# A hybrid decoder layer on one core: seven products for every pair of the MLP's second product, 13 pairs' weight sums made earlier, source order from the 19th early product

## The chip, the core and the metric

The kernel runs on one NeuronCore of a Trainium2 chip. The metric is device microseconds of one execution. TensorE (PE) does the matrix products, VectorE (DVE), ScalarE (ACT) and GpSimd (POOL) the elementwise work, and SyncE (SP) issues all DMAs of this kernel in one queue. PEld is the loading of TensorE's stationary operand.

## What is computed

One decoder layer on x (1024 tokens x 1024 features, float32): an input projection, a dilated attention in three head groups beside an RWKV-7 time mixing, a gated merge of the two with an output projection, and then, where the change mostly lies, a squared-ReLU MLP, with RMSNorm before and after each part:

```python
f = rmsnorm(h, ffn_pre_norm[i])
f = jnp.square(jax.nn.relu(f @ w_ff_in[i])) @ w_ff_out[i]      # 1024x1024 @ 1024x4096, then @ 4096x1024
h = h + rmsnorm(f, ffn_post_norm[i])
e = (p[i] @ w_ple[i]) * jax.nn.sigmoid(h @ w_ple_gate[i])
h = h + rmsnorm(e, ple_post_norm[i])
```

## The kernel before, in words

**Products in three passes.** A float32 operand x is split into a rounded high part and the rest: ACT copies x into a reduced-precision tile (the "high"), and DVE or POOL subtracts it from x (the "low"). A product is then high x high + high x low + low x high, three matmuls (`mm3`, lines 310, 312 and 314). So each operand costs one ACT copy and one subtraction beside PE's work, and a "low" is a subtraction of 128x512 elements with both inputs in SBUF.

**Stages, in order of time.** (1) the input projection and the RWKV recurrence; (2) the attention, whose chain of scores (`sc`), row maxima and exponentials (DVE writes `SB` and `ast`, ACT does the exp), transposes (`pt`), copies (`PB`) and values (`po`) runs through 24 rounds, while PE fills the time between with the input projection's remaining products (`z<-uh,wh`); (3) `combine` of the three groups and the `merge` of eight column blocks; (4) the output projection (`out_0`, `out_1`); (5) 32 "early" products of the MLP's first product (`early`), with preparation beside them (`beside`); (6) the pairs; (7) the tail: the last part of the second product, the embedding gate, the output.

**The pairs.** The MLP's inner width of 4096 is cut into NP = 16 pairs of 128 features (256 rows of w_ff_out each). In stage 6, loop index p runs from 1 to 15. In each step PE does the first product of pair p (five products of 12 matmuls, in 20 chunks of three, function `first`; tiles `z`), and between these chunks the second product of pair e = p-1. Its 2x2 blocks are multiplied in one of two ways. For even e, `seven`: seven products of block sums in place of eight (84 matmuls), accumulated in PSUM banks (`chain`), each of whose four banks DVE adds into the totals `tot` after each product: 28 evictions. For odd e, `plain`: all eight block products (96 matmuls), summed two by two in PSUM: 16 evictions. `seven` needs sums of blocks of its activations (`operand`, four DVE subtractions or additions of tile `hr` into tile `sum`), and sums of blocks of its weights. The weight sums of a pair are four DVE operations, then split (four ACT copies, four DVE lows) and stored in DRAM scratch (`bs`, 512 KB each, 4 for each pair); `fetch` loads them into `duo` when they are due. The pairs in `AHEAD = (4, 2, 0)` have them made beside the early products (`ahead_`), the other even ones beside the plain pair in front of them (`w2_sums` in the loop). In a plain pair DVE also makes four lows of the activations (`duo<-hr`), and ACT and POOL split the whole weights (`ws`).

Each step of the loop also loads one pair's w_ff_out rows (`load_w2`), the four blocks of the next w_ff_in pair (`w1_raw`), and the early products from scratch (`take`, tile `hr`), and POOL makes four sums of blocks of w_ff_in (`w1_sum`; tiles `wr`, `wl`) and five lows (`w1_split`). In plain pairs it also converts weights for the tail (`part`: tile `gp`, one DVE low and two stores for each of 28 halves).

**What sets the order.** PE's instructions are in source order throughout; a planner (`Order`) that runs while the program is written chooses when each generator of work goes on. It has a clock of its own, and spawned generators come in when it has passed the time that they yielded. For the other engines, `tc.manual_schedule(engines=...)` keeps source order while it is entered; outside it, the framework's scheduler orders their instructions. Before the change, all from the attention to the end of stage 5 is outside it (SP alone is in source order in stage 5), and all engines are in source order from the start of stage 6. `pend` and `flush` hold small jobs, lows above all, back to the next chunk.

**Buffers.** A tile is allocated by tag, and a new tile of the same tag waits until the old one is no longer read. The tag MP holds one 512 KB tile, BK2 a 1 MB one. PSUM has eight banks: s0, z0, z1 for `z`, and s1, s2, s3, m0, m1 for the rest; `bank(tags)` takes them in turn.

## Time and profile before

| | us |
|---|---|
| median of 3 runs (lowest to highest) | 1753.67 (1752.29 to 1756.36) |
| the profiled execution itself | 1755.44 |
| its span in the trace | 1753.7 |
| PE busy, DVE busy, ACT busy, POOL busy | 1727.1, 1108.6, 736.9, 606.0 |

The stages by the trace: the first attention transposes stand at 530.2, the merge's first product with the attention's result at 821.6, the output projection starts at 883.8, the early products at 974.4, the pairs at 1098.1, and the tail at 1608.4. A row of a group tells the line (118 is the helper that records every elementwise operation, so tiles tell more than lines), the engine, the operation, output tiles <- input tiles, the shape and the count, then busy time and the mean of one in ns, then the engine's idle time before them and who ended it. A row of the timeline tells the start and the duration in us, then the same, and in brackets the idle time before it. A row of the windows tells each engine's busy time in a stretch, the granted clock of TensorE as a share, the DMA engines' busy share and GB/s.

### The profile page before, as it was taken

The numbers are of one execution on the slowest core, as the hardware profiler recorded it, in microseconds if no ns is written. First come the engines' busy times: TensorE is split into PE (matmuls) and PEld (weight loads), VectorE is DVE, ScalarE is ACT, GpSimd is POOL, SyncE is SP. The second block draws the span as 40 slices with busy tenths as digits, with TensorE's granted clock in tenths as the row PEclk, the third lists the DMA queues.
The fourth block names the chain that finished last, engine by engine and source line by source line (L and its number), as shares of the span: only waits on it lengthen the run. The fifth ranks groups of instructions, "written<-read, shape, count | busy, mean of one in ns | idle before, by whom it ended". The sixth has DMA issues, their size and how long they took to land.

```text
span 1753.7 us, 26435 instructions
## 1 busy us (share of the span) xinstructions
PE 1727.1 (98%) x10132; PEld 1409.0 (80%) x10132; DVE 1108.6 (63%) x1926; ACT 736.9 (42%) x1353; POOL 606.0 (35%) x393
## 2 busy tenths in 40 slices
PE   9999999999999999999999998999999999999998
PEld 8777888887887777777788876888888888888887
DVE  6377778677654333445746752766788788787643
ACT  5823333241424443453444555333433443443354
POOL 1121110121122322323230346656656756752311
PEclk9999999999999999999999999999999999999999
DMA  4521121221333222234533386364464665567611
GB/s 164 214 84 37 67 79 62 84 73 63 107 115 107 85 61 61 73 117 147 192 100 120 120 334 237 129 219 157 145 245 175 203 223 174 194 225 273 221 49 49
DMA packets 99968, 244.77 MB, mean 140 GB/s; under 512 B 11393, under 2 KB 11777, under 8 KB 99330
## 3 DMA queue, kind: packets, MB, share of 16 engines
q1 hardware_dynamic: 99842, 243.08, 40.3%
q8 instruction: 80, 1.31, 0.3%
q14 instruction: 46, 0.38, 0.1%
HBM read 169.24 MB, written 67.11 MB: 135 GB/s over the span
## 4 chain that ended last, share of the span: by engine, by line
PE 80%; DVE 7%; ACT 4%; DMA 4%; issue 2%; POOL 2%; SPq 1%; DVEq 0%; ACTq 0%; POOLq 0%
PE z L310 15%; PE z L314 15%; PE z L312 15%; PE bk L310 8%; PE bk L314 8%; PE bk L312 8%; PE tp L301 1%; PE sc L293 1%; PE A L293 1%; PE po L293 1%; PE pt L301 1%; PE wr L293 1%; PE fq L293 1%; DVE duo L118 1%; POOL wl L118 1%
## 5 line engine op out<-in xcount | busy, mean ns | idle before, releaser
L118 POOL TENSOR_TENSOR wl<-wr,wh 128x1024 fp32r<-128x1024 f32 (+1 forms) x56 | 133.3, 2382 | 589.8 <-ACT wh L118 584.4
L310 PE MATMUL z<-uh,wh 128*128 128x512 f32 (+1 forms) x800 | 313.4, 392 | 4.0 <-DVE v L118 3.2
L312 PE MATMUL z<-ul,wh 128*128 128x512 f32 (+1 forms) x800 | 312.6, 391 | 1.3 <-DVE ul L118 1.3
L314 PE MATMUL z<-uh,wl 128*128 128x512 f32 (+1 forms) x800 | 312.9, 391 | 0.7 <-POOL wl L118 0.7
L118 DVE TENSOR_TENSOR tot<-tot,bk 128x512 f32<-128x512 f32 x333 | 219.6, 681 | 82.3 <-PE bk L314 82.1
L310 PEld LDWEIGHTS z<-uh,wh 128*128 128x128 f32 x800 | 151.0, 189 | 36.0 <-issue 4.9
L314 PEld LDWEIGHTS z<-uh,wl 128*128 128x128 f32 x800 | 151.1, 189 | 31.8 <-issue 3.7
L312 PEld LDWEIGHTS z<-ul,wh 128*128 128x128 f32 x800 | 151.1, 189 | 31.7 <-issue 3.3
L118 ACT ACTIVATE wh<-wr 128x1024 fp32r<-128x1024 f32 (+2 forms) x94 | 81.0, 862 | 119.5 <-PE z L312 65.9
L118 ACT ACTIVATE hr<-hr 128x512 f32<-128x512 f32 x96 | 60.7, 632 | 134.8 <-DVE hr L118 133.3
L310 PE MATMUL bk<-duo 128*128 128x512 f32 x224 | 88.4, 395 | 0.3
L312 PE MATMUL bk<-duo 128*128 128x512 f32 x224 | 87.7, 392 | 0.0
L314 PE MATMUL bk<-duo 128*128 128x512 f32 x224 | 87.5, 391 | 0.0
L314 PE MATMUL bk<-ws,duo 128*128 128x512 f32 x224 | 87.1, 389 | 0.0
L310 PE MATMUL bk<-ws,duo 128*128 128x512 f32 x224 | 87.1, 389 | 0.0
L312 PE MATMUL bk<-ws,duo 128*128 128x512 f32 x224 | 87.1, 389 | 0.0
L118 ACT ACTIVATE duo<-sum 128x512 fp32r<-128x512 f32 x64 | 39.7, 628 | 112.4 <-DVE sum L118 100.5
L310 PE MATMUL z<-f,wh 128*128 128x512 f32 x212 | 83.1, 392 | 3.5 <-ACT pa L118 3.5
L314 PE MATMUL z<-f,wh 128*128 128x512 f32 x212 | 83.4, 393 | 1.3 <-POOL wh L118 1.3
L312 PE MATMUL z<-f,wh 128*128 128x512 f32 x212 | 83.0, 391 | 0.0
L118 POOL TENSOR_TENSOR wh<-wr,wh 128x512 fp32r<-128x512 f32 x38 | 54.5, 1437 | 81.2 <-ACT wh L118 81.2
L118 DVE TENSOR_TENSOR hr<-hr,z 128x512 f32<-128x512 f32 x80 | 54.5, 681 | 23.4 <-PE z L314 23.3
(371 smaller groups left out, 4009.2 us busy)
## 6 DMA issues: line engine op xcount, KB each, us to landing
wr<-in_wz_dram SPq DMA_DIRECT2D x48, 512.0 KB, 4.0
w2r<-in_w_ff_dram SPq DMA_DIRECT2D x34, 512.0 KB, 4.5
bs<-duo SPq DMA_DIRECT2D x32, 512.0 KB, 4.8
duo<-bs SPq DMA_DIRECT2D x32, 512.0 KB, 4.3
wr<-in_wff_dram SPq DMA_DIRECT2D x56, 256.0 KB, 3.6
hr<-p1scr SPq DMA_DIRECT2D x48, 256.0 KB, 4.1
xt<-in_x_dram SPq DMA_DIRECT2D x16, 512.0 KB, 3.9
gscr<-gst SPq DMA_DIRECT2D x32, 256.0 KB, 2.2
```

Source lines behind the costliest of these rows:

```text
L118: return f(*a, **kw)
L293: PE.matmul(out_, a, b, start=start, stop=stop)
L301: PE.transpose(out_, a, ident if idn is None else idn)
L310: PE.matmul(ps, ah, bh, start=start and i == 0, stop=False, skip_group_check=not start)
L312: PE.matmul(ps, ah, bl, start=False, stop=False, skip_group_check=not start)
L314: PE.matmul(ps, al, bh, start=False, stop=i == n - 1, skip_group_check=not start)
```

## The change

All pairs 0 to 14 of the second product are done by `seven`; `plain`, its weights' split and its branch of the loop are gone. So weight sums are needed for 15 pairs, not 8. `AHEAD` is now (1, 0): these two are made beside the early products. The other 13 (`SOONER`, pairs 2 to 14) are made by a new generator, `sooner`, which runs beside the attention. It loads each pair's two rows blocks again into one BK2 tile, and has 52 steps, for which it asks the planner for 5.0 us each (`PACE`): one or two DVE sums, one ACT copy into a tile of tag MP, one DVE low and one store of 512 KB. It writes to the engines directly, so that the planner's account of DVE's and ACT's time does not hold these operations. The tiles `rooms` for operands go round three pairs of buffers without a break. `part` comes twice in each step. Source order for DVE, ACT, POOL and SP begins at the 19th early product (j = 18), not at the first pair. In the early products' preparation, lows are made at once or at the end of the step. In `merge`, the blocks from j = 2 on take turns in four PSUM banks in place of two.

```diff
-LEAD, SPARE, LAG, HELD = 0.4, 0.5, 0.4, 2.5
+LEAD, SPARE, LAG, HELD, PACE = 0.4, 0.5, 0.4, 2.5, 5.0
...
         yield from wait(lambda: ("P", NU - 1, 1) in done)
         in_turn.__exit__(None, None, None)
         V.shared = False
+        sch.spawn(sooner(), 2)
...
-                ps = bank(("s1", "s2"))
+                ps = bank(("s1", "s2") if j < 2 else ("s1", "s2", "m0", "m1"))
...
+    AHEAD, SOONER = (1, 0), tuple(range(2, NP - 1))
...
-    bs_scr = {(p, i): dram.tile([128, 2, 512], F32, name=f"bs{p}_{i}") for p in range(0, NP - 1, 2) for i in (6, 5, 7, 4)}
+    bs_scr = {(p, i): dram.tile([128, 2, 512], F32, name=f"bs{p}_{i}") for p in range(NP - 1) for i in (6, 5, 7, 4)}
...
-        lo() if j < NA else pend.append(lo)
+        lo() if k is not None else pend.append(lo)
...
-    AHEAD = (4, 2, 0)
...
         if j == 18:
             yield from wait(lambda: 7 in t_f)
+            last["turn"].__exit__(None, None, None)
+            last["turn"] = tc.manual_schedule(engines=OTHERS)
+            last["turn"].__enter__()
...
+        if j < NA:
+            flush()
...
-        last["turn"].__exit__(None, None, None)
-        last["turn"] = tc.manual_schedule(engines=OTHERS)
-        last["turn"].__enter__()
         prep(0)
         prep(1)
...
         for p in range(1, NP):
             Y["n"] = 0
             e = p - 1
-            if e % 2 == 0:
...
-            for u in range(8):
-                if u % 2 == 0:
-                    flush()
-                    part(2 * p - 4 + u // 2, 0)
-                yield from chunks((20 * u + 23) // 8)
...
-                yield from plain(items.index((e, u // 2)), u % 2)
...
+            if e:
+                fetch(e, 5)
+            for x in range(7):
+                yield from chunks((20 * x + 23) // 7 if p < NP - 1 else (3, 6, 9, 13, 17, 20, 20)[x])
+                yield from seven(items.index((e, x)))
+                if x in (0, 3) and p < NP - 1:
+                    part(units[0], 0)
+                if x in (2, 5) and p < NP - 1:
+                    part(units.pop(0), 1)
+                if x == 2:
+                    load_w2(p)
+                if x == 4:
+                    take(p + 1)
...
+    def sooner():
+        raws = {}
+
+        def load(i):
+            raws[i] = rtile([128, 2, 1024], "w2e", "BK2")
+            for k in (0, 1):
+                nc.sync.dma_start(raws[i][:, k], row(w_ff2, 2 * SOONER[i] + k))
+
+        def minus(out_, a, b):
+            nc.vector.tensor_tensor(out_, a, b, OP.subtract)
+
+        load(0)
+        yield 8.0
+        for i, p in enumerate(SOONER):
+            b = [raws[i][:, x // 2, halves[x % 2]] for x in range(4)]
+            t1, t2 = (rtile([128, 512], "sum", x) for x in ("pg", "yc"))
+            for x in range(4):
+                if x == 0:
+                    minus(t1, b[1], b[0])
+                    minus(t2, b[3], t1)
+                if x == 2:
+                    minus(t1, b[3], b[1])
+                    minus(t2, b[2], t2)
+                    if i + 1 < len(SOONER):
+                        load(i + 1)
+                t = (t2, t1, t1, t2)[x]
+                d = rtile([128, 2, 512], "duo", "MP", F32R)
+                nc.scalar.activation(d[:, 0], t, AF.Copy)
+                minus(d[:, 1], t, d[:, 0])
+                nc.sync.dma_start(bs_scr[p, (6, 5, 7, 4)[x]], d.bitcast(F32))
+                yield PACE
+        done.add("sooner")
...
     def rooms(e):
-        r = (("Ep", "En"), ("a", "px"), ("kk", "v"))
-        return (r[1], r[0], r[2]) if e // 2 % 2 else r
+        r = (("Ep", "En"), ("kk", "v"), ("a", "px"))
+        return r[e % 3:] + r[:e % 3]
...
-    items = [(e, x) for e in range(NP - 1) for x in range(4 if e % 2 else 7)]
+    items = [(e, x) for e in range(NP - 1) for x in range(7)]
```

The order of the instructions, engine by engine, shows what moves. PE's order is the same as before up to the first pair; from there it has 84 matmuls fewer. The first place is DVE's queue in one of the last rounds of the attention, before. An ISA row is the masked row maximum of one head's scores (its second half hands out the accumulator), `nm` the scaled maximum that the exponential takes, `PB` the copy of transposed weights that the values wait for:

```order
L118 ISA SB,ast<-sc,amask 128x256
L118 ISA ast 128x1
L118 ISA SB,ast<-sc,amask 128x256
L118 ISA ast 128x1
L118 TENSOR_SCALAR nm<-ast 128x2 x2
L118 COPY PB<-pt 128x512 x2
```

The same place on DVE now, with the operations of `sooner` (line 1784; `w2e` are its weights, `sum` its sums, `duo` its splits):

```order
L118 ISA SB,ast<-sc,amask 128x256
L118 ISA ast 128x1
L118 TENSOR_SCALAR nm<-ast 128x2
L118 ISA SB,ast<-sc,amask 128x256
L118 ISA ast 128x1
L1784 TENSOR_TENSOR sum<-w2e 128x512
L118 TENSOR_SCALAR nm<-ast 128x2
L1784 TENSOR_TENSOR duo<-sum,duo 128x512
L1784 TENSOR_TENSOR sum<-w2e,sum 128x512
L118 COPY PB<-pt 128x512 x2
```

One sum now stands between the last maximum and its `nm`, and a low (which reads what ACT copied) and a sum stand between `nm` and the copies.

The second place is POOL's queue at the end of stage 5 and the start of the pairs, before. `wh<-wa` is the low of an early product's weights, `wr`, `wl` and `wh<-wr` are sums and lows of the first product's weights, `duo` are lows of the second product's operands:

```order
L118 TENSOR_TENSOR wh<-wa,wh 128x512
L118 TENSOR_TENSOR duo<-sum,duo 128x512
L118 TENSOR_TENSOR wl<-wr,wl 128x512
L118 TENSOR_TENSOR wr<-wr 128x512
L118 TENSOR_TENSOR wr<-wl,wr 128x512
L118 TENSOR_TENSOR wl<-wl 128x512
L118 TENSOR_TENSOR wr<-wr 128x512
L118 TENSOR_TENSOR wh<-wr,wh 128x512 x2
L118 TENSOR_TENSOR duo<-sum,duo 128x512
```

And POOL's queue there now:

```order
L118 TENSOR_TENSOR wh<-wa,wh 128x512
L118 TENSOR_TENSOR wl<-wr,wl 128x512
L118 TENSOR_TENSOR wr<-wr 128x512
L118 TENSOR_TENSOR wh<-wa,wh 128x512
L118 TENSOR_TENSOR wh<-wr,wh 128x512
L118 TENSOR_TENSOR wl<-wl 128x512
L118 TENSOR_TENSOR duo<-hr,duo 128x512
L118 TENSOR_TENSOR duo<-w2r,duo 128x512
L118 TENSOR_TENSOR duo<-sum,duo 128x512
```

The lows of the pairs' operands now stand behind the lows and sums that the last early products and the first chunks need; before, one `duo` low (with two more just above it) stood in front of them, and the sums in front of `wh<-wr`.

More of the change, by code (lines that the diff above doesn't have):

```diff
@@ L1380, in body @@
             if i == 0:
+                assert "sooner" in done
                 gn["f"] = rtile([128, D], "gn", "kk")
@@ L1605, in early @@
         SY.dma_start((p1_scr if i == 1 else c_scr)[p], dst)
-    AHEAD = (4, 2, 0)
-    steps = [(0, -1), (0, 0), (1, -1)] + [(0, n) for n in range(1, 6)] + [(1, 0), (2, -1)] + [
-        (1, n) for n in range(1, 6)] + [(2, n) for n in range(6)]
+    steps = [(0, -1), (0, 0), (1, -1)] + [(0, n) for n in range(1, 6)] + [(1, n) for n in range(6)]
     def ahead_(n):
@@ L1719, in mlp @@
             e = p - 1
-            if e % 2 == 0:
-                if e:
-                    fetch(e, 5)
-                for x in range(7):
-                    yield from chunks((20 * x + 23) // 7 if p < NP - 1 else (3, 6, 9, 13, 17, 20, 20)[x])
-                    yield from seven(items.index((e, x)))
-                    if x == 2:
-                        load_w2(p)
-                    if x == 6 and p < NP - 1 and p + 1 not in AHEAD:
-                        load_w2(p + 1)
-                    if x == 4:
-                        take(p + 1)
-                    if p == NP - 1:
-                        if x == 0:
-                            last_w(0, "BT")
-                            last_w(1, "BK2")
-                        if x in (2, 4, 5):
-                            e_weights((2, 4, 5).index(x))
-                        if x == 4:
-                            last_split(0, (0, 1))
-                        if x == 5:
-                            last_split(1, (1, 0))
-                continue
@@ L1918, in seven @@
             flush()
-    def plain(n, part):
-        e, x = items[n]
-        if part == 0:
-            prep(n + 2)
-        m, c = 1 - x // 2, x % 2
-        a, (hi, lo) = duo[e, m], ops["w"]
-        for t in (2 * part, 2 * part + 1):
-            ts = slice(t * 128, t * 128 + 128)
-            ps = bank(XB)
-            yield from mm3(ps, [(a[j][:, 0, ts], a[j][:, 1, ts], hi[:, j, halves[c]], lo[:, j, halves[c]])
-                                for j in range(2)])
-            V.tensor_tensor(tot[m][c][:, t], tot[m][c][:, t], ps, OP.add)
-            flush()
     gp = {}
```

62 lines of the change are left out of this document (21 added, 41 removed).

## The prediction

> **What bounds the kernel now.** I read the page first: one engine is busy nearly all the time.
>
> ```profile
> PE 1727.1 (98%) x10132; PEld 1409.0 (80%) x10132; DVE 1108.6 (63%) x1926; ACT 736.9 (42%) x1353; POOL 606.0 (35%) x393
> ```
>
> Busy is not yet bound, so the windows by stage come next: attention, early products, pairs, one seven pair, one plain pair, and six microseconds at the start of the pairs.
>
> ```profile
> 530.00:821.00 291.00, 290.49 (x1637) 223.88 (x1636) 118.31 (x357) 129.19 (x295) 89.36 (x37) 1.00 0.29 87
> 974.00:1098.00 124.00, 115.94 (x536) 93.99 (x535) 56.88 (x69) 72.37 (x134) 64.16 (x47) 0.98 0.66 242
> 1098.00:1603.00 505.00, 504.65 (x2213) 415.39 (x2212) 397.84 (x529) 196.09 (x342) 314.31 (x232) 1.00 0.56 191
> 1166.50:1199.00 32.50, 32.45 (x144) 26.54 (x143) 25.26 (x35) 10.89 (x20) 24.19 (x18) 1.00 0.50 170
> 1199.50:1234.00 34.50, 34.50 (x154) 28.59 (x153) 23.38 (x30) 13.05 (x23) 18.73 (x14) 1.00 0.53 176
> 1094.00:1100.00 6.00, 5.08 (x12) 4.01 (x13) 0.41 (x1) 0.41 (x1) 3.33 (x3) 0.50 0.50 162
> ```
>
> PE's busy column is full in the attention and in the pairs; only the early products lose 8.1 us of 124, and behind them the granted clock is 0.50. So PE's own work sets the end, and a matmul that is left out counts in full, at its price per start. The group's mean is not that price, since matmuls overlap:
>
> ```profile
> L310 PE MATMUL bk<-duo 128*128 128x512 f32 x224 | 88.4, 395 | 0.3
> ```
>
> The timeline of PE gives the step: two starts 68.38 us apart, one seven pair and one plain pair later.
>
> ```profile
> 1128.19 0.39 PE L314 MATMUL bk<-duo 128*128 128x512 f32 x1
> 1128.62 0.50 PE L310 MATMUL bk<-duo 128*128 128x512 f32 x1
> ...
> 1196.56 0.39 PE L314 MATMUL bk<-duo 128*128 128x512 f32 x1
> 1197.00 0.50 PE L310 MATMUL bk<-duo 128*128 128x512 f32 x1
> ```
>
> Between 1128.62 and 1197.00 stand 60+84 and 60+96 matmuls, 300 in all. One start in them comes 0.44 us behind the one before (1196.56 to 1197.00), and the next is 0.1 us late too; without this 0.33 us a matmul takes 68.05/300 = 0.2268 us.
>
> **The change part by part.** *Fewer matmuls.* Seven plain pairs (e = 1, 3 to 13) go from 96 to 84: 84 x 0.2268 = 19.0 us less, all on the bound engine.
>
> *DVE and POOL in the pairs.* These groups are of 1112 to 1600 us, DVE first:
>
> ```profile
> L118 DVE TENSOR_TENSOR tot<-tot,bk 128x512 f32<-128x512 f32 x310 | 204.8, 681 | 81.0 <-PE bk L314 80.9
> L118 DVE TENSOR_TENSOR hr<-hr,z 128x512 f32<-128x512 f32 x72 | 49.0, 681 | 7.1 <-PE z L314 7.1
> L118 DVE TENSOR_TENSOR duo<-hr,duo 128x512 fp32r<-128x512 f32 x28 | 44.4, 1625 | 7.7 <-ACT duo L118 7.3
> L118 DVE TENSOR_TENSOR gp<-gp,gph 128x512 fp32r<-128x512 f32 x28 | 28.4, 1014 | 2.6 <-ACT gph L118 2.6
> L118 DVE TENSOR_TENSOR sum<-hr 128x512 f32<-128x512 f32 x14 | 16.4, 1171 | 1.0 <-ACT hr L118 0.8
> L118 DVE TENSOR_TENSOR sum<-sum,hr 128x512 f32<-128x512 f32 x7 | 11.7, 1668 | 0.2
> ```
>
> ```profile
> L118 POOL TENSOR_TENSOR duo<-sum,duo 128x512 fp32r<-128x512 f32 x29 | 37.6, 1297 | 19.7 <-ACT duo L118 19.7
> L118 POOL TENSOR_TENSOR wr<-wr 128x512 f32<-128x512 f32 x28 | 39.0, 1395 | 1.1
> ```
>
> Each step now lasts 144 x 0.2268 = 32.7 us on PE. DVE has in it 28 evictions and 5 `hr` at 0.681 (22.5), 4 sums at 1.2 to 1.7 (5.0 by these rows, counting the fourth like the first) and 2 `gp` at 1.0: 29.5 us, 90%. POOL has 10 operand lows, 5 lows and 4 sums of first-product weights, 19 at 1.30 to 1.40: 24.7 to 26.6 us, 81%. The seven pair above ran with DVE at 25.3 and POOL at 24.2 of 32.5 and lost nothing but the 0.33 us at its end, where DVE was held by two `duo<-hr` lows of the plain pair to come. These are gone: 7 x 0.33 = 2.3 us less. A bank is written again 21 matmuls after its last product ended, 4.8 us; less its 0.7 us eviction, DVE may be late by 4 us before PE feels it. Two sums in a row, at 1.7 each, stay inside. I charge 0.1 us a step for bunches, 1.5 us in all; the ends are 0 and the DVE-POOL rival below. Fetches of weight sums, now four in every step, start two products (9.5 us) ahead; DMA share stays near the plain pair's 0.53.
>
> *The start of the pairs.* The timeline of PE there:
>
> ```profile
> 1089.04 0.39 PE L314 MATMUL bk<-f,wh 128*128 128x512 f32 x1
> 1092.90 0.50 PE L310 MATMUL z<-f,wh 128*128 128x512 f32 x1 [3.47 <-ACT pa L118]
> 1093.23 0.40 PE L312 MATMUL z<-f,wh 128*128 128x512 f32 x1
> 1094.92 0.79 PE L314 MATMUL z<-f,wh 128*128 128x512 f32 x1 [1.28 <-POOL wh L118]
> ...
> 1098.07 0.63 PE L310 MATMUL bk<-duo 128*128 128x512 f32 x1
> ```
>
> From 1089.27, the next start that was due, to 1098.07 lie 8.8 us for nine `z` matmuls of 2.04: 6.8 us lost, and about 1.1 more until the clock is back near 1100. Why, POOL's timeline tells: it waited with a `duo` low of the coming pairs in front, and the first product's sums behind it.
>
> ```profile
> 1085.93 1.29 POOL L118 TENSOR_TENSOR duo<-sum,duo 128x512 fp32r<-128x512 f32 x1 [2.79 <-ACT duo L118]
> 1087.18 1.29 POOL L118 TENSOR_TENSOR wl<-wr,wl 128x512 f32<-128x512 f32 x1
> ```
>
> Source order puts these lows last. That has a price: behind the last early product ACT does `pa` twice, then two `duo` copies, and POOL two lows, before the pair's second matmul. ACT's steps follow each other like this:
>
> ```profile
> 1092.27 0.58 ACT L118 ACTIVATE pa<-bk 128x512 f32<-128x512 f32 x1
> 1092.75 0.62 ACT L118 ACTIVATE wh<-wr 128x512 fp32r<-128x512 f32 x1
> ```
>
> The third step ends 0.5 + 0.5 + 0.62 = 1.6 us behind the product, two lows of 1.30 end at 4.2, or 4.3 with a hop; the nine `z` matmuls cover 2.04, so PE waits about 2.3 us. So 7.9 - 2.3 = 5.6 us less. The clock fell behind 3.47 us of idle time; whether it does behind 2.3 the rows leave open, and a drop would cost the 1.1 us again. [...]
>
> *The early products.* PE's waits from 1000 to 1110, besides the 3.5 and 1.3 above:
>
> ```profile
> PE bk L314 <- POOL wh L118: 2.1, 2, 1.7
> PE bk L314 <- POOL wl L118: 0.6, 1, 0.6
> ```
>
> The 1.7 has first-product sums in POOL's queue ahead of the low that PE needs; source order mixes them, and two pairs' sums are prepared there in place of three. I take half of 2.7 plus restarts: 1.6 us less (0 to 3.2).
>
> *Merge.* Two waits, from 820 to 884:
>
> ```profile
> PE bk L310 <- DVE g L118: 0.8, 1, 0.8
> PE bk L310 <- ACT wh L118: 0.8, 1, 0.8
> ```
>
> Four banks in place of two take the first away: 0.8 us less. The last steps of `sooner` fall into the combine before it.
>
> *The attention.* `sooner` puts 104 DVE operations, 52 ACT copies and 78 DMAs of 512 KB (41 MB) into 291 us. DVE is busy for 118 and ACT for 129 of them, so there is room; what counts is latency in front of PE. One round, of three engines' timelines:
>
> ```profile
> 666.67 0.29 DVE L118 CUSTOM_DVE_ANT_0 SB<-sc,amask 128x128 f32<-128x128 f32 x1 [0.16 <-PE sc L293]
> ...
> 669.66 0.19 ACT L118 ACTIVATION_READ_ACCUMULATOR SB<-SB,nm 128x1 f32 x1
> ...
> 671.23 0.88 PE L301 MATMUL pt<-cs,SB 128*128 128x128 f32 x6
> ```
>
> The exponentials end at 669.85 and PE comes to the transposes at 671.23: 1.4 us to spare. PE's order is fixed, so anything over that is a wait. In the new order about nine of 24 rounds have one `sooner` operation inside this chain on DVE, two rounds have two, and some have an ACT copy (0.62) in it. A DVE operation with two SBUF inputs takes 0.69 us with POOL idle,
>
> ```profile
> 1084.49 0.69 DVE L118 TENSOR_TENSOR sum<-sum,hr 128x512 f32<-128x512 f32 x1
> ```
>
> and up to 1.67 with POOL at work (the group above). POOL is busy for 89 of the 291 us: 1.0 in the mean. Two rounds lose 2.0 + 0.62 - 1.4 = 1.2 us and nine 1.0 + 0.62 - 1.4 = 0.2: 4 us, and I add 3 for steps in which the store buffer is late: 7 us, between 0 and the 36 of the first rival.
>
> *Sum.* -19.0 - 2.3 + 1.5 - 5.6 - 1.6 - 0.8 + 7 = -20.8 us. Against the profiled execution's 1755.4 that is 1734.6; its time stands 1.8 above the median of 1753.67, so the median should become 1733.
>
> **The rivals.** *The store buffer paces the attention (slower).* All 52 steps go through one MP tile: ACT's copy must wait until the last store has been read out. A step is then landing + 0.62 + a DVE low of 0.7 to 1.7. The attention has 291/52 = 5.6 us for each.
>
> ```profile
> DMA to landing us min/median/max: 2.9/4.5/7.5
> ...
> wr<-in_wz_dram SPq DMA_DIRECT2D x19, 512.0 KB, 3.7
> ```
>
> The first row is for all stores and loads of weight sums (`bs`) elsewhere, the second a load of its size in the attention. At 3.7 a step is 5.3 and fits. At the median of 4.5 with 1.2 for the low it is 6.3: 0.7 x 52 = 36 us late, on queues in which the exponentials stand behind these copies. Then the sum is -27.8 + 36 = +8, 1762. It decides for slower from 5.6 + 27.8/52 = 6.1 us a step. For it: the stage gets 41 MB in 291 us, 140 GB/s, on top of its 87. Against: the buffer rarely meets other stores here, and the 2.9 was seen with few about.
>
> *DVE and POOL keep each other out in the pairs.* If each of DVE's six two-input operations waits for a whole POOL operation (1.30 + 0.69 = 1.99), DVE needs 22.5 + 11.9 = 34.4 us a step, 1.7 more than PE: 14 x 1.7 = 24 us, and the sum is +1.7, 1755. It begins at a mean of 1.70; the rows above reach 1.668 in one group and 1.0 to 1.2 in the others. [...]
>
> *Attention costs 15 to 22* in small waits, at the same mechanism as in my sum: 1741 to 1748.
>
> *More is gained:* attention free, all early waits gone: -19 - 2.3 - 7.9 - 3.2 - 1.6 = -34, 1720.
>
> **How the numbers follow.** A change of 0.2% (3.5 us) is about what a measurement of this kernel can tell. Forecast (1726 to 1741) 0.60; more gained (1719 to 1726) 0.12; attention dear 0.14; store buffer 0.08 (1757 to 1775); DVE-POOL 0.06 (1740 to 1757). The range 1721 to 1749 leaves out the store buffer, half of DVE-POOL and part of the best case, under 0.2. Slower is the store buffer, 0.08; no change, two thirds of DVE-POOL, 0.04; faster, the rest, 0.88.
>
> **What would show it.** Right: 84 fewer `bk` matmuls, steps of 32.7 to 32.9 us between equal points of the pairs, under 3 us of waits at their start with the clock at 1.00, waits on `SB` from ACT or `nm` in the attention of some microseconds. Wrong: steps of 33 us or more with PE waiting for `tot`; ACT's `duo` copies of the attention waiting for DMA; a wait over 3.4 us at the start of the pairs.

## The result and the profile after

The changed kernel takes 1774.35 us (median of 4 runs, 1771.73 to 1775.77), where the kernel before takes 1752.98 (4 runs): a ratio of 1.0118, 95% interval 1.0106 to 1.0130. It is 21 us slower; forecast were 21 us faster. Its profiled execution took 1771.73 us, with a span of 1770.0. It is the fastest of the four, so the two traces lie 16.3 us apart, not 21.

The starts of the stages in the two traces (first instruction of PE for the tiles named in the section on the profile of before) say where:

| stage, us | before | after | difference | forecast |
|---|---|---|---|---|
| attention, to the merge's first `z<-oah` | 291.4 | 339.7 | +48.3 | +7 |
| merge | 62.2 | 60.7 | -1.5 | -0.8 |
| output projection | 90.7 | 91.4 | +0.7 | 0 |
| early products, to the first pair | 123.6 | 114.0 | -9.6 | -7.2 |
| pairs, to the tail | 510.3 | 489.2 | -21.1 | -19.8 |

The rest differs by 0.5 us. So four stages came within 2.4 us of the forecast, and the attention lost 48 us. The windows of the kernel after (columns as in the prediction): the attention in the same 291 us and whole, the early products, the pairs, and six microseconds at their start.

```profile
530.00:821.00 291.00, 259.36 (x1422) 199.81 (x1421) 176.11 (x408) 135.95 (x309) 73.40 (x29) 0.94 0.53 185
530.00:869.00 339.00, 306.05 (x1636) 234.38 (x1635) 208.16 (x461) 158.10 (x347) 87.13 (x37) 0.94 0.55 193
...
1021.00:1135.00 114.00, 112.75 (x534) 92.86 (x533) 48.79 (x61) 69.42 (x128) 58.08 (x43) 1.00 0.63 227
1135.00:1600.00 465.00, 463.77 (x2046) 383.66 (x2046) 387.19 (x552) 187.72 (x327) 362.37 (x273) 1.00 0.63 213
1132.00:1138.00 6.00, 4.08 (x17) 2.73 (x17) 0.10 (x1) 4.34 (x8) 4.73 (x4) 1.00 0.36 131
```

Before, PE was busy for 290.5 of the first 291 us; now for 259.4, no engine is full, and the granted clock is 0.94 in the mean. Over the whole stage the same matmuls keep PE busy for 306.1 us in place of 290.5: some 16 of the 48 us are matmuls at a lower clock behind the waits, and the rest is the waits themselves. What PE waited for there (us in total, times, longest):

```profile
PE sc L293 <- DVE qk L118: 24.1, 5, 8.2
PE po L293 <- DVE PB L118: 4.0, 4, 2.1
PE cb L293 <- DVE OTA L118: 1.2, 1, 1.2
PE rc L301 <- DVE row L118: 1.2, 2, 0.7
PE pt L301 <- ACT vkb L118: 1.0, 2, 0.7
PE pt L301 <- ACT SB L118: 0.8, 1, 0.8
```

Before, this list was empty. 24.1 of its 32.3 us are not in the rounds at all. They stand in five places: in front of the first scores of a group, which need q and k with the rotary turn. That chain is: ACT copies the second half of the keys out of PSUM, four small transfers on SP swap rows into `sw`, POOL multiplies `sw` and DVE multiplies `qk` by the rotary table, DVE adds. Before, at the first of the five places, SP, DVE, POOL and PE:

```profile
561.25 2.42 SPq L137 DMA_DIRECT2D sw<-qk  x4
```

```profile
569.04 1.22 DVE L118 TENSOR_TENSOR qk<-qk,sw 128x1024 f32<-128x1024 f32 x1 [2.29 <-POOL sw L118]
```

```profile
565.56 3.44 POOL L118 TENSOR_TENSOR sw<-sw,rope 128x1024 f32<-128x1024 f32 x1 [1.01 <-DMA sw<-qk]
```

```profile
571.88 0.72 PE L293 MATMUL sc<-qk 64*128 64x128 f32 x8
```

The sum ends at 570.26 and the scores start at 571.88: 1.6 us of slack (1.6, 0.7, 0.8, 1.3 and 2.0 us at the five places). The same place after, SP first:

```profile
564.22 1.15 SPq L137 DMA_DIRECT2D sw<-qk  x2
568.10 0.33 SPq L1804 DMA_DIRECT2D bs<-duo  x1
568.49 1.17 SPq L137 DMA_DIRECT2D sw<-qk  x2
```

```profile
565.60 2.47 DVE L1784 TENSOR_TENSOR duo<-sum,duo 128x512 fp32r<-128x512 f32 x1 [3.95 <-ACT duo L1802]
...
572.41 2.86 DVE L1784 TENSOR_TENSOR sum<-w2e 128x512 f32<-128x512 f32 x1
575.20 3.36 DVE L118 TENSOR_TENSOR qk<-qk,rope 128x1024 f32<-128x1024 f32 x1
578.66 1.23 DVE L118 TENSOR_TENSOR qk<-qk,sw 128x1024 f32<-128x1024 f32 x1
```

```profile
565.13 2.39 POOL L118 TENSOR_TENSOR wl<-wr,wh 128x1024 fp32r<-128x1024 f32 x1 [15.89 <-ACT wh L118]
572.31 2.41 POOL L118 TENSOR_TENSOR sw<-sw,rope 128x1024 f32<-128x1024 f32 x1 [4.79 <-DMA sw<-qk]
574.79 2.68 POOL L118 TENSOR_TENSOR wl<-wr,wh 128x1024 fp32r<-128x1024 f32 x1
```

```profile
579.94 1.22 PE L293 MATMUL sc<-qk 64*128 64x128 f32 x8 [5.02 <-DVE qk L118]
```

Three things add up. A store of the new sums stands on SP between the second and the third rotary transfer and goes out at 568.10, when its low ends. That low takes 2.47 us in place of 0.69: POOL started a `wl` 0.5 us before it, and the low ends 0.55 us behind that `wl`. And when the transfers have landed, a new sum stands in front of the rotary product, again beside POOL: it ends at 575.27, 0.55 us behind POOL's operation. So the product begins 2.8 us late and itself meets POOL's next `wl` (3.36 us in place of 1.23). PE waits 5.0 us here, and the scores start 8 us later than before; the other 3 had been lost earlier in the stage.

The first of the three is at all five places: a store stands on SP between the rotary transfers, and the next of them goes out 3.1, 6.5, 1.3, 2.4 and 2.8 us behind the end of the one before it. In the trace of the kernel before the transfers of a group go out in a row, with nothing between them.

### The profile page after: what moved, and what is told of

The parts are those of the page before. It is cut to its first block, busy times and chain, and to the rows that moved or that the text cites. A ratio compares the mean times of both kernels' runs of the same rounds, so it can differ in the third digit from the quotient of the medians.

```text
span 1770.0 us, 26759 instructions
## 1 busy us (share of the span) xinstructions
PE 1716.1 (97%) x10048; PEld 1401.2 (79%) x10048; DVE 1194.3 (67%) x2066; ACT 761.4 (43%) x1395; POOL 655.8 (37%) x435
## 4 chain that ended last, share of the span: by engine, by line
PE 76%; DVE 10%; ACT 5%; DMA 5%; issue 3%; POOL 1%; SPq 0%; DVEq 0%; ACTq 0%; POOLq 0%
PE z L314 13%; PE z L312 13%; PE z L310 13%; PE bk L310 8%; PE bk L312 8%; PE bk L314 8%; DMA bs<-duo 2%; DVE duo L1784 1%; PE tp L301 1%; DVE qk L118 1%; DMA g<-gscr 1%; ACT SB L118 1%; PE A L293 1%; PE wr L293 1%; PE fq L293 1%
## 5 line engine op out<-in xcount | busy, mean ns | idle before, releaser
L118 DVE TENSOR_TENSOR tot<-tot,bk 128x512 f32<-128x512 f32 x417 | 273.0, 682 | 54.2 <-PE bk L314 54.1
L312 PEld LDWEIGHTS z<-ul,wh 128*128 128x128 f32 x800 | 152.9, 191 | 32.3 <-issue 3.5
L312 PE MATMUL bk<-duo 128*128 128x512 f32 x420 | 163.5, 389 | 1.2 <-POOL duo L118 1.2
L310 PE MATMUL bk<-duo 128*128 128x512 f32 x420 | 163.4, 389 | 0.0
L314 PE MATMUL bk<-duo 128*128 128x512 f32 x420 | 163.4, 389 | 0.0
L118 ACT ACTIVATE hr<-hr 128x512 f32<-128x512 f32 x96 | 60.7, 633 | 129.4 <-DVE hr L118 127.9
L118 POOL TENSOR_TENSOR duo<-sum,duo 128x512 fp32r<-128x512 f32 x60 | 84.1, 1402 | 51.4 <-ACT duo L118 51.4
L1784 DVE TENSOR_TENSOR duo<-sum,duo 128x512 fp32r<-128x512 f32 x52 | 46.5, 894 | 71.9 <-ACT duo L1802 71.8
L312 PEld LDWEIGHTS bk<-duo 128*128 128x128 f32 x420 | 78.8, 188 | 18.0 <-POOL duo L118 1.7
L310 PEld LDWEIGHTS bk<-duo 128*128 128x128 f32 x420 | 78.9, 188 | 16.6 <-ACT wl L118 0.2
L314 PEld LDWEIGHTS bk<-duo 128*128 128x128 f32 x420 | 78.9, 188 | 16.3
L310 PE MATMUL z<-f,wh 128*128 128x512 f32 x212 | 82.6, 390 | 0.7 <-ACT pa L118 0.7
L312 PE MATMUL z<-f,wh 128*128 128x512 f32 x212 | 82.5, 389 | 0.0
```

The source lines that it names most:

```text
L118: return f(*a, **kw)
L310: PE.matmul(ps, ah, bh, start=start and i == 0, stop=False, skip_group_check=not start)
L312: PE.matmul(ps, ah, bl, start=False, stop=False, skip_group_check=not start)
L314: PE.matmul(ps, al, bh, start=False, stop=i == n - 1, skip_group_check=not start)
L1784: nc.vector.tensor_tensor(out_, a, b, OP.subtract)
```

## The experiments

Three theories were put to the test. *S, the store*: there is one buffer, so ACT's next copy waits for the store's end (S1), and SP's queue holds what stands behind a store that waits for its low (S2). *Q, the queues of DVE and ACT*: the new operations stand in front of others, and POOL makes them longer. *M, the traffic*: the bytes themselves. The table has the attention stage of each run by its trace, and its time; a time without an interval is that of a single execution. `no_sooner`, `traffic`, `small_sums`, `no_stores` and `late_order` leave out work that the layer needs: they tell what that work costs and are no kernels to use.

| run | attention, us | time, us | ratio to before, 95% interval |
|---|---|---|---|
| before (medians beside these runs; one execution of 1757.65 beside the two late_sp) | 291.4 | 1753.0 to 1754.6 | |
| changed kernel | 339.7 | 1774.35 | 1.0118 (1.0106 to 1.0130) |
| no_sooner | 291.1 | 1722.0 | |
| traffic | 290.6 | 1722.3 | |
| small_sums | 295.0 | 1726.6 | |
| no_stores | 311.4 | 1743.7 | |
| planned | 334.5 | 1774.1 | 1.0116 (1.0096 to 1.0136) |
| three_slots; again, slots_timed | 316.4; 318.4 | 1748.2; 1753.6 | 0.9999 (0.9989 to 1.0008) |
| pool_queue | 350.7 | 1790.1 | |
| slots_pool | 360.6 | 1794.0 | |
| slots_pool_gated | 356.2 | 1793.7 | 1.0223 (1.0204 to 1.0242) |
| round_turn | 324.4 | 1765.3 | 1.0056 (1.0041 to 1.0071) |
| round_one | 324.5 | 1772.9 | |
| dve_turn_gate | 321.6 | 1766.4 | 1.0073 (1.0056 to 1.0090) |
| dve_turn_free | 320.2 | 1761.4 | 1.0045 (1.0030 to 1.0060) |
| late_sp | 339.6 | 1780.0 | |
| late_sp_only | 349.8 | 1785.1 | |
| late_order | 291.4 | 1727.1 | |
| order_only | 291.0 | 1748.8 | 0.9975 (0.9965 to 0.9986) |

PE's order in the attention is that of the changed kernel in all of them but `planned` and `order_only` (there it is that of before, which is the same).

### Taking parts of the added work away

```diff
-        sch.spawn(sooner(), 2)
+        done.add("sooner")
...
-        SY.dma_start(b.bitcast(F32), bs_scr[e, i])
+        SY.dma_start(b.bitcast(F32), bs_scr[e % 2, i])
```

This is `no_sooner`, with the operands of the pairs loaded from the sums of pairs 0 and 1. Expected was:

> Leaves out the sums of weights of pairs 2 to 14 beside the attention altogether (their operands are loaded from the sums of pairs 0 and 1), so it is the rest of the change alone. If the loss is the new work in the attention and nothing else, the attention stage (first av transposes to the merge's first z<-oah) is back at 291 us from 340, and the time is 1774 - 48 = 1726. If the order of the rest (source order from the 19th early product, four banks in the merge) has a part in it, the stage stays above 296 us.

```diff
-                nc.sync.dma_start(bs_scr[p, (6, 5, 7, 4)[x]], d.bitcast(F32))
                 yield PACE
```

This is `no_stores`, with the same loads of operands. Expected was:

> Leaves out the 52 stores of sums beside the attention; their loads, DVE sums and lows and ACT copies stay. Theory S (the store: its one buffer, and its place in SP's queue ahead of the rotary transfers): the attention falls from 340 us to under 305. Theory Q (DVE and ACT have the new operations in front of the rotary chain, and POOL holds DVE up): it stays above 325. Both alike: near 315.

```diff
+        d = rtile([128, 2, 512], "duo", "MP", F32R)
+        nc.vector.memset(d.bitcast(F32), 0.0)
...
             for x in range(4):
...
+                if x == 2 and i + 1 < len(SOONER):
+                    load(i + 1)
                 nc.sync.dma_start(bs_scr[p, (6, 5, 7, 4)[x]], d.bitcast(F32))
                 yield PACE
```

This is `traffic`, in which the sums, copies and lows are gone too. Expected was:

> Leaves out all DVE and ACT operations of the sums beside the attention; the 26 loads and 52 stores stay, the stores from a constant tile, so that no store waits for anything. If the bytes themselves or the number of transfers hold the rotary transfers up (theory M): the attention stays over 310 us. If it is waiting in front of the stores (S) or the operations (Q): under 297.

```diff
-            nc.vector.tensor_tensor(out_, a, b, OP.subtract)
+            nc.vector.tensor_tensor(out_[:, 0:16], a[:, 0:16], b[:, 0:16], OP.subtract)
```

This edit on `no_stores` is `small_sums`; its two tiles of sums are filled once, ahead of the loop. Expected was:

> The run without stores, with the 104 sums and lows on DVE narrowed from 512 to 16 columns (their place in the queue, their waits and the 52 full copies on ACT stay). Without stores the attention took 311 us, 20 more than with nothing. If these 20 us are DVE's time (Q: operations of 0.7 to 2.9 us in front of maxima, nm and copies), the attention falls under 297 us and the time under 1729. If they are ACT's copies of 0.63 us in front of the exponentials, or the waits between the engines, it stays over 305.

Without `sooner` the attention is back at 291 us and the time at 1722.0, 32 us below the 1754.2 measured beside it: the loss is the added work and nothing else. M falls as a cause by itself: 26 loads and 52 stores that wait for nothing cost nothing (290.6 us). Without the stores alone, 28 of the 48 us are gone, and the waits move from the start of a group into the rounds:

```profile
PE pt L301 <- ACT SB L118: 8.0, 10, 2.2
PE sc L293 <- DVE qk L118: 1.9, 2, 1.3
```

With DVE's operations narrowed as well (the groups of `no_stores`, then of `small_sums`), 16.4 of the other 20 go:

```profile
L1784 DVE TENSOR_TENSOR duo<-sum,duo 128x512 fp32r<-128x512 f32 x52 | 50.2, 965 | 29.4 <-ACT duo L1802 29.3
```

```profile
L1784 DVE TENSOR_TENSOR duo<-sum,duo 128x16 fp32r<-128x16 f32 x52 | 16.6, 319 | 36.9 <-ACT duo L1804 36.5
```

So the 48 us, taken away in this order, are 28 for the stores, 16 for DVE's time and 4 for ACT's copies and the rest. These are not shares at a fixed order, since the framework's scheduler orders the engines other than PE anew in each version. By the two traces 66 of some 360 operations of DVE in the stage stand in another order in `small_sums` than in `no_stores`, so their place in the queue did not stay, as the expectation has it. What part of the 28 and the 16 is the new order itself was not tested.

### Letting the planner know

```diff
-            nc.vector.tensor_tensor(out_, a, b, OP.subtract)
+            V.tensor_tensor(out_, a, b, OP.subtract)
...
-                nc.scalar.activation(d[:, 0], t, AF.Copy)
+                S.activation(d[:, 0], t, AF.Copy)
```

This is `planned`. Expected was:

> The same work, but its operations go through the planner's accounts, so that PE's order puts the scores later where the planner sees DVE and ACT taken. If the loss is that PE's fixed order did not know of the new operations (Q, with PE free to do other products meanwhile): the attention falls by 15 us or more, to under 325, and the time to under 1759. If the waits are in what the planner doesn't see (the store's buffer, SP's queue, POOL's hold on DVE): within 8 us of 340.

The loads and stores go through the planner's `SY` too. PE's order moves, the attention shortens by 5 us, the merge is 6 us longer, and the time stays. PE still waits 18.9 us for `qk`. That agrees with the second branch of the expectation: the planner's account holds durations, not a store's buffer or a DVE operation that lasts longer beside POOL (2.47 us in place of 0.69 above).

### The buffer and the queue of the stores

```diff
+        slots = (d[:, 0], d[:, 1], rtile([128, 512], "duo", "yc", F32R))
...
+                hi, lo = slots[n % 3], slots[(n + 1) % 3]
+                nc.scalar.activation(hi, t, AF.Copy)
+                nc.sync.dma_start(bs_scr[p, (5, 6, 7, 4)[x]][:, 0], hi.bitcast(F32))
+                minus(lo, t, hi)
+                nc.sync.dma_start(bs_scr[p, (5, 6, 7, 4)[x]][:, 1], lo.bitcast(F32))
```

This is `three_slots`. Expected was:

> The splits beside the attention rotate through three half buffers (two of the one tile, one that the sums made in place have freed), and highs and lows are stored by themselves as soon as they are made, one sum a step; stores stay in SP's queue. If the single buffer is what the stores cost (S1), ACT's copies no longer wait for transfers and the attention falls from 340 us to under 320. If it is SP's queue (S2), the lows' stores still stand ahead of the rotary transfers: over 328.

```diff
-                nc.sync.dma_start(bs_scr[p, (6, 5, 7, 4)[x]], d.bitcast(F32))
+                nc.gpsimd.dma_start(bs_scr[p, (6, 5, 7, 4)[x]], d.bitcast(F32))
```

This is `pool_queue`. Expected was:

> The 52 stores beside the attention go through POOL's queue in place of SP's; all else is as in the changed kernel. If what the stores cost is their place in SP's queue ahead of the rotary transfers (S2: a store there waits for its low on DVE), most of the 28 us that leaving them out gave comes back: the attention falls from 340 us to under 320. If it is the single buffer (S1: ACT's next copy waits for the store's end, and what stands behind it on ACT waits too), it stays over 330. POOL now waits in front of a store for the low; if that matters, the rotary multiplication on POOL comes later and the attention is longer than 340.

The next run, `slots_pool`, has both edits at once. Expected was:

> Both of these at once. If S1 and S2 are the whole of what the stores cost, the attention is near the 311 us that it has without stores, and the time near 1744; if transfers or POOL's waits cost something of their own, over 318.

And the last one, `slots_pool_gated`, a gate besides:

```diff
+                    done.add("rot")
...
+            done.discard("rot")
...
+                yield from wait(lambda: "rot" not in done)
```

Expected was:

> Both, and no step of the sums begins between the second half of a group's keys and the group's first scores. If the 20 us that are left without stores come from DVE and ACT operations in front of the rotary chain (Q), the attention is under 303 us and the time under 1735. If they come from the rounds of scores, exponentials and transposes (the waits for SB in the run without stores: 8.0 us in 10 times), it stays over 306.

Three half buffers take 23 us off the attention, most of what leaving the stores out takes. By the expectation this is S1. But the expectation took for granted that stores would still stand ahead of the rotary transfers, and at the place that was shown above the four now go out in a row:

```profile
566.29 2.42 SPq L137 DMA_DIRECT2D sw<-qk  x4
```

So it is at every group of this run, and of its repetition `slots_timed`. The edit also spreads the sums, one to a step. It takes away the wait for the buffer and the stores between the rotary transfers at once, and does not tell S1 from S2. In the changed kernel ACT stood for 34.6 us in front of the copies `duo`, waiting for the store, though a store landed in 2.8 us:

```profile
L1802 ACT ACTIVATE duo<-sum 128x512 fp32r<-128x512 f32 x52 | 32.6, 628 | 43.4 <-DMA bs<-duo 34.6 <-DVE sum L1784 8.6
```

```profile
bs<-duo SPq DMA_DIRECT2D x52, 512.0 KB, 2.8
```

With three half buffers the first scores of a group wait 1.3 us in all, as without stores, and what is left stands in the rounds again:

```profile
PE pt L301 <- ACT SB L118: 9.2, 6, 2.6
PE rc L301 <- DVE row L118: 1.6, 1, 1.6
PE sc L293 <- DVE qk L118: 1.3, 1, 1.3
```

The single execution of 1748.2 us flattered it: 11 executions of `slots_timed`, the same kernel, give 1747.6 to 1757.7 and a median of 1753.6, no different from before. For this repetition was expected:

> The version with three half buffers once more, timed against the kernel before: 1746 to 1750 us, 0.3 to 0.5 per cent faster than before, if its one look was typical.

POOL's queue is worse by 11 us in the attention than SP's. POOL's own row shows why: it stands in front of the stores for the lows (the last figures), and its rotary products and weight lows stand behind.

```profile
POOL bs L1804 <- DVE duo L1784: 134.8, 34, 7.2
```

On SP the rotary transfers go out in a row there, too. So moving the queue does not test S2 cleanly: it puts the same wait in front of another link of the same chain. The gate, which keeps sums out of that chain, brings 4 us of the attention back there and nothing of the time.

### Other orders

Here DVE and ACT (round_turn, round_one), DVE alone (dve_turn_gate, dve_turn_free) or DVE and SP (late_sp) keep source order through the attention, and a step of the sums is let go behind a round's maxima. The gate on the rotary chain (`rot`) is in round_turn, round_one and dve_turn_gate. All have three half buffers but round_one, which has the one buffer. In late_sp and late_sp_only (SP alone in source order) the stores and the next load are written down 2.5 us behind a step.

```diff
+        att_turn = tc.manual_schedule(engines={mybir.EngineType.DVE, mybir.EngineType.Activation})
+        att_turn.__enter__()
...
+                yield from wait(lambda: "rot" not in done and (go[0] > used[0] or not inside[0]()))
+                used[0] = go[0]
```

In late_sp and late_sp_only, with the engines of the first line changed:

```diff
+                yield 2.5
+                for k, half in enumerate((hi, lo)):
+                    nc.sync.dma_start(bs_scr[p, (5, 6, 7, 4)[x]][:, k], half.bitcast(F32))
+                if x > 1:
+                    load(i + 1, x - 2)
+                yield PACE - 2.5
```

`round_turn`, DVE and ACT in source order. Expected was:

> Three half buffers as before (stores in SP's queue), and DVE and ACT in source order through the attention: in a round of scores one step of the sums stands right behind the two scaled maxima (DVE) and the four exponentials (ACT), outside the rounds by time and not between a group's last key half and its first scores. PE's order is the same. If the 25 us that three half buffers leave over are sums and lows in front of nm and the exponentials (Q), the attention falls from 316 us to under 300 and the time to about 1730, faster than both kernels. If they come from POOL holding DVE up, or from transfers, whatever the order, it stays over 308 and the time over 1740.

`round_one`, the same with one buffer:

> The same source order with the one buffer of the changed kernel. If the single buffer costs through ACT's queue wherever the copies stand (S1), the attention is 15 to 30 us longer than with three half buffers in this order. If it costs only where the order puts copies ahead of the rotary chain, under 8 us longer.

`dve_turn_gate`, DVE alone:

> Three half buffers; DVE alone in source order through the attention (ACT and POOL are ordered by the scheduler again), one step of the sums in a round behind its maxima, two to three between the rounds and none between a group's last key half and its first scores; steps asked for 4 us apart there, so that the last stand before the merge. In the run with DVE and ACT in source order the rounds of scores lost nothing, but the rotary chain waited for POOL behind a weight's low (9.7 us), and the steps in the merge cost 10 us. If those two came from ACT's order and from the late steps, both go: attention under 300 us, merge near 60, time under 1735. If sums and lows cost wherever they stand on DVE, the attention stays over 310 us and the time over 1742.

`dve_turn_free`, without the gate:

> The same without the gate at the start of a group: steps come 5 us apart between the rounds, also in front of the rotary operations. If what costs at the start of a group is any DVE work beside the rotary chain (its slack was 0.7 to 2.0 us before the change), it is 4 to 10 us slower than with the gate, in waits of the scores for the rotated q and k. If the chain only suffered from ACT's waits for the one buffer, the two are within 3 us of each other.

`late_sp`, DVE and SP:

> Three half buffers, DVE in source order without the gate, and now SP too in source order through the attention: the stores and the next load of a step are written down 2.5 us behind its DVE operations, so that they do not stand in SP's queue before what they wait for is done. The run with DVE alone in source order had 11.8 us of waits of the scores for the rotated q and k, in two places where SP held a small rotary transfer for 4 to 6 us behind a store. If that order of SP's queue (S2) is their cause, these waits fall under 4 us, the attention from 320 to about 308 us and the time to about 1750. If it is DVE work in front of the rotary chain, they stay.

`late_sp_only`, SP alone, with no step held for a round:

> Three half buffers, DVE and ACT ordered by the scheduler as in the run that gave 1748 us, SP in source order with the stores 2.5 us late. If SP's queue still cost something in that run (its rotary waits were 1.3 us only), the time falls below 1745; if what is left there comes from DVE's clusters of sums in a round (waits for SB of 9.2 us), it stays within 4 us of 1748.

None of these brought the gain that was hoped for. In round_turn the waits for `SB` are gone, as Q says, but others took their place, in the rotary chain, at `PB` and in the merge (69.7 us, 7.5 more than in the kernel before), since 13 of the 52 copies now start only behind the attention:

```profile
PE sc L293 <- DVE qk L118: 9.7, 5, 2.8
PE po L293 <- DVE PB L118: 5.4, 3, 2.8
PE bk L310 <- ACT wh L118: 3.8, 1, 3.8
```

round_one speaks against S1 as a price of its own. In this order the one buffer costs the attention 0.2 us (324.5 against 324.4) and some 7 us in the whole, of which 5.7 stand in the merge and the output projection, since 15 of its steps start only behind the attention. Yet ACT stood there for 30.8 us of the attention in front of copies that waited for a store, nearly as long as in the changed kernel. What is missing is the other wait: where a store stands between its rotary transfers, the next goes out 0.7 us later, not 1.3 to 6.5. So these two runs point to S2 for the larger part of the 23 us. As the order changed as well, this is argued and not shown. The gate was expected to gain 4 to 10 us over dve_turn_free and lost 5. (The two also differ in the pace that is asked for, 4 us against 5.) The steps that it holds back fall into the merge (73.8 us against 65.2), and two waits of 11.0 and 6.6 us for `qk` remained. In the longer, SP held rotary transfers behind stores. In the other the rotary transfers took 6.9 us to land, where 2.3 is the median of this stage in the kernel before: a load of 512 KB for the sums went out between them, and the 16 DMA engines were busy at 98 to 100% from 714 to 720. Behind that a weight's low stood on POOL ahead of the rotary product. So the bytes, which cost nothing in `traffic`, may have cost something here, where a load fell beside these transfers. dve_turn_free has one place of the first kind:

```profile
611.08 0.51 SPq L137 DMA_DIRECT2D sw<-qk  x1
611.68 0.53 SPq L1819 DMA_DIRECT2D bs<-duo  x1
613.12 0.33 SPq L1821 DMA_DIRECT2D bs<-duo  x1
613.49 0.43 SPq L1789 DMA_DIRECT2D w2e<-in_w_ff_dram  x1
615.65 0.32 SPq L1819 DMA_DIRECT2D bs<-duo  x1
616.39 0.32 SPq L1821 DMA_DIRECT2D bs<-duo  x1
616.77 1.78 SPq L137 DMA_DIRECT2D sw<-qk  x3
```

The second rotary transfer is issued 5.7 us behind the first; that is S2 in a trace, as at the five places of the changed kernel. With SP in source order (late_sp) the waits for `qk` fall from 11.8 to 4.3 us, but now loads of weights stand behind the stores, and PE waits for the weights instead:

```profile
PE z L314 <- POOL wl L118: 6.8, 5, 2.5
PE po L293 <- DVE PB L118: 5.9, 3, 3.8
PE sc L293 <- DVE qk L118: 4.3, 5, 1.4
```

S2 is thus seen in the traces and not isolated: each run that changed SP's order put another wait in its place. No order that was tried brings the attention under 316 us with the sums and their stores in it.

### The small parts by themselves

```diff
-            last["turn"].__exit__(None, None, None)
-            last["turn"] = tc.manual_schedule(engines=OTHERS)
-            last["turn"].__enter__()
         if j == 21:
...
+        last["turn"].__exit__(None, None, None)
+        last["turn"] = tc.manual_schedule(engines=OTHERS)
+        last["turn"].__enter__()
         prep(0)
```

This is `late_order`; the edit is on no_sooner. Expected was:

> Leaves out the sums beside the attention as the first of these runs did, and puts the start of source order back to the first pair; all else is of the changed kernel. If source order from the 19th early product is what gained at the start of the pairs, the stretch from the first early product to the first pair is 5 to 10 us longer than the 114 us it has now, and PE's waits for pa and wh are back. If the early stage gained by having two pairs' sums beside it in place of three, or by lows made at once, it stays within 3 us of 114.

The early stage takes 119.4 us in place of 114.1: source order from the 19th early product is worth 5.3 us there. The pairs behind it take 487.6 in place of 489.3, mostly since the wait of 1.2 us for a `duo` low at their start belongs to that order. Both together leave 3.6 us. The waits are back as expected (4.1 us for `wh`, 1.2 for `pa`), but not at their old size: the 3.5 us for `pa` and the fall of the clock to 0.50, which the kernel before has at the first pair, are gone without source order too (granted clock 1.00). The other 4.2 us that the stage gained against 123.6 come from the lows and the two pairs' sums.

The last version is the kernel before with these small parts alone:

```diff
-                ps = bank(("s1", "s2"))
+                ps = bank(("s1", "s2") if j < 2 else ("s1", "s2", "m0", "m1"))
...
-        lo() if j < NA else pend.append(lo)
+        lo() if k is not None else pend.append(lo)
...
             yield from wait(lambda: 7 in t_f)
+            last["turn"].__exit__(None, None, None)
+            last["turn"] = tc.manual_schedule(engines=OTHERS)
+            last["turn"].__enter__()
...
+        if j < NA:
+            flush()
```

This is `order_only`. Expected was:

> The kernel before, with only the small parts of the change: source order from the 19th early product, lows of the early products at once or at the end of the step, four banks in the merge. Seven and plain pairs alternate as before, three pairs' sums beside the early products, nothing new beside the attention. If the small parts are worth the same without the rest (the run with source order from the first pair was 5.3 us longer at the start of the pairs), the time is 1754 less 5 to 11, about 1745, and that is faster than before. If they only help where fewer sums are made there, within 2 us of before.

Of the versions that do all of the layer's work, it is the only one that beats both kernels: 1748.8 us (8 executions, 1746.2 to 1751.4), 0.25% less than before and 4 us more than the 1745 that was expected. Its early stage takes 116.6 us and its merge 59.9, in the trace of the fastest of the eight. With three pairs' sums beside it, the early stage is 2.6 us longer than the 114.0 of the changed kernel with two.

## Why the prediction was wrong, point by point

- **Fewer matmuls, no stalls: right.** -19.8 us forecast, -21.1 measured. The 1.5 us for bunches did not come: from 1135 to 1600 PE was busy for 463.8 of 465 us, and 1.2 of the rest is the wait at the first pair. DVE was at 387 of 465 (83%; forecast 90%), POOL at 78% (81%). The rival of DVE and POOL keeping each other out in the pairs did not occur: it begins at a mean of 1.70 us for the six sums and `gp` lows of a step, and they took 1.06 in the mean from 1135 to 1600.
- **Start of the pairs: right in what it looks like, not wholly in the cause.** Forecast were about 2.3 us of waits and a clock that stays up. The second was an estimate: the trace of before has the clock at 0.50 behind a wait of 2.70 us (from 152 to 154) and at 1.00 behind one of 1.66 us (at 1044), and nothing between these. PE's waits there, 1.9 us, with the granted clock at 1.00:

```profile
1133.34 0.50 PE L310 MATMUL z<-f,wh 128*128 128x512 f32 x1 [0.69 <-ACT pa L118]
...
1137.13 0.50 PE L312 MATMUL bk<-duo 128*128 128x512 f32 x1 [1.23 <-POOL duo L118]
```

  Source order by itself is worth 3.6 us (5.3 in the early stage, less 1.7 in the pairs), where the forecast had 5.6 with its price taken off: the other small parts, with two pairs' sums in place of three, had already taken away the longest wait and the fall of the clock. What these parts gain was undersized: 1.6 us forecast for the early waits, 4.2 measured; so was the merge, 0.8 against 2.4 without the sums. That the early stage came out near the forecast (-9.6 against -7.2) is in part two errors that cancel.
- **The attention: the step that failed.** 7 us were forecast, 48 measured. It was priced as one round: "1.4 us to spare. PE's order is fixed, so anything over that is a wait", and gave 4 us of waits in the rounds plus 3 for a late store. The rounds behaved so in the changed kernel (0.8 us for `SB`, 4.0 for `PB`). But the stage has a second chain in front of PE, the rotary one, with 0.7 to 2.0 us of slack, that goes through ACT, SP, POOL and DVE in turn. The prediction does not name it, and it holds 24.1 of the 32.3 us of waits. Nor was the clock counted: its mean over the stage fell to 0.94 behind the waits, some 16 us more.
- **The price of a DVE operation** was right in the mean (1.0 forecast; 100.5 us by 104 = 0.97), but its upper end was not: 1.67 us came from a stage where POOL's operations are 512 wide. In the attention they are 1024 wide and last 2.4 us, and the sums and lows beside them lasted up to 2.86. In the trace of the changed kernel 80 of the 104 ran with POOL idle and 5 began 0.4 to 0.6 us ahead of a POOL operation: these 85 took 0.68 to 0.69 us. The other 19 began while POOL was at work; they took 1.02 to 2.86 us, and each ended 0.54 to 0.56 us behind POOL's operation. So the length of POOL's operations in the stage in question set the upper end. It went the other way, too: at six places in the kernel before, POOL's rotary product started 0.03 or 0.04 us behind a DVE product of 1.23 us and took 3.44 or 3.45 us in place of 2.4.
- **The rival of the store buffer** had 0.08, 1762 us, and 1757 to 1775 for its range, in which the measured time just lies; that is luck, as its mechanism was another. Its sign came: ACT's `duo` copies waited 34.6 us for DMA. Its condition seems met: the 52 stores were issued from 540.2 to 864.4, 6.4 us apart, over the 6.1 named. But a stage of 340 us spaces 52 steps by 6.5 whatever holds it up, so this does not show a pace. That the stores cost is right, since leaving them out gives 28 us back. How they cost is not: it reckoned with late landings (4.5 us) as a pace, and they took 2.8. By the traces they cost through what stood behind them: the rotary transfers behind the waiting store at all five places. What ACT's waiting copies held up was not isolated. The 3 us that the sum took for late stores should have been near 28.

## What to carry to other kernels

Room on an engine says nothing about work that is put beside a fixed order: list every chain that ends in front of the bound engine, with the slack of each and every queue that it passes through (the DMA queue too), and price the new work against the smallest slack. Here stores that stood on SP before their lows were ready held rotary transfers back by 1.3 to 6.5 us, and ACT stood for 34.6 us in front of copies whose buffer was not free. What such a wait costs is set by what is queued behind it: in one order, 30.8 us of ACT's waits for the buffer cost the stage 0.2 us. An edit that leaves work out lets the scheduler order the rest anew, so compare the orders before the difference is put down to the work. A gain that is certain (fewer matmuls) and its price (where the operands are made) are worth measuring apart: here the small parts alone beat the whole, by 26 us.

## What the runs showed of the hardware that was not expected

The clock fell behind two short waits. In the changed kernel, windows of 2 us from 660:

```profile
660.00:662.00 2.00, 1.96 (x15) 1.46 (x12) 0.72 (x1) 1.25 (x5) 1.60 (x1) 1.00 0.03 8
662.00:664.00 2.00, 1.07 (x5) 0.56 (x3) 1.97 (x3) 1.08 (x1) 0.79 (x1) 1.00 0.00 0
664.00:666.00 2.00, 1.39 (x13) 0.98 (x14) 2.00 (x4) 0.25 (x1) 0.00 (x0) 0.94 0.97 299
666.00:668.00 2.00, 2.00 (x6) 1.52 (x6) 1.90 (x3) 1.29 (x2) 0.00 (x0) 0.50 0.56 225
668.00:670.00 2.00, 2.00 (x8) 1.56 (x7) 0.74 (x2) 0.00 (x0) 0.00 (x0) 0.71 0.58 240
```

From 660 to 666 PE was idle for 1.6 us of six, 1.5 of them in two pieces (1.38 and 0.16) within 2 us. The clock then read 0.50 from 666 to 669, with matmuls starting 0.43 us apart in place of 0.23, and 1.00 again from 670. A wait of 2.70 us ends near 151 in both traces: behind it the clock read 0.50 in the kernel before and 1.00 in the changed one. At the start of the pairs PE was idle for more, 1.9 us of six, in waits of 0.7 and 1.2 us with 2.6 us of matmuls between them, and the clock stayed at 1.00. So the idle time of six microseconds does not decide by itself; what does, these runs leave open.
